# Mixture of 32 experts behind an attention layer: the widest and the narrowest expert visited last instead of second

## The chip, the cores and the metric

One core of a Trainium2 chip runs the whole layer as one program. The metric is device time in microseconds (us) of one execution; lower is better. The engines are named as in the profile: PE (TensorE matmuls), PEld (its weight loads), DVE (VectorE), ACT (ScalarE), POOL (GpSimd), SP (SyncE, which issues most DMAs).

## What is computed

A decoder layer for 1024 tokens of width 1024: an input projection, grouped attention beside a gated MLP, an output projection, then a mixture of experts. The change touches only the mixture:

```python
logits = (xt @ w_router + b_router).astype(jnp.float32)
top_val, top_idx = lax.top_k(logits, TOP_K)          # 4 of 32 experts for each token
gate = jax.nn.softmax(top_val, axis=-1)
...
def expert_block(args):
    e, tok, g = args
    xb = x_pad[tok]
    h = xb @ w_gate_up[e] + b_gate_up[e]             # 1024 -> 2048, columns interleaved
    h_glu = jnp.minimum(h[:, 0::2], SWIGLU_LIMIT)
    h_lin = jnp.clip(h[:, 1::2], -SWIGLU_LIMIT, SWIGLU_LIMIT)
    a = h_glu * jax.nn.sigmoid(SWIGLU_ALPHA * h_glu) * (h_lin + 1.0)
    return ((a @ w_down[e] + b_down[e]) * g[:, None]).astype(x.dtype)
...
y = jnp.zeros((N + 1, D), x.dtype).at[tok_buf].add(out.reshape(P, D))
```

Each token's four results are added onto its row of the output. All weights are float32 in HBM, 12 MB for each expert.

## The kernel before

**Rooms.** Experts are ranked by how many tokens chose them, on the device. The program is fixed, so the expert of rank r gets a room of `ROOM[r]` columns: 320 for rank 0, 256 for rank 1, then 240, 232, 208 and so on down to 72 for rank 30 and 64 for rank 31; 160 at rank 12, 152 at 13 and 14, 136 at 15 to 17, 120 at 19. Below, "expert 0" is the expert of rank 0. The number of the expert itself is read from a table when its weights are loaded. (A loop behind the last expert takes tokens that found no room; it makes no pass here.)

**Two streams.** `visits` (line 37) makes two lists: ranks 0 to 15 as the wide stream, ranks 31 down to 16 as the narrow one; from each it takes the element at place `FIRST = 12` (expert 12, room 160, and expert 19, room 120) and puts it first. So the wide stream is 12, 0, 1, 2, ..., 11, 13, 14, 15, and the narrow one 19, 31, 30, 29, ..., 20, 18, 17, 16. An expert is six products, four with the gate-up weights ("gu") and two with the down weights ("dn"); `pieces` (line 1925) lists them for a stream, with the next expert's first gu ahead of the present one's dn. `seq` (line 1934) takes products from the two streams by turns, the wide one three products ahead, so the last three products of the program are of the narrow stream's last expert.

**One product.** It has two halves. For each, SP loads 1 MB of weights into one of five float32 buffers (`raw`, line 1773; four of them are called xw in the trace), ACT writes the float16 high part wh (line 1780), DVE the low part wl (line 1783), into one of six buffers (`ws`). PE then does 48 matmuls for the half, four blocks of 12 (lines 1826 to 1828): wh by the two halves of x, wl by one, with as many columns as the room has. Accumulators sit in six PSUM banks. Behind a gu block DVE clamps (line 1841), ACT applies the gelu (1846), DVE multiplies (1849), ACT writes the high half of `a` (1852) and POOL the low half by a subtraction (1854); the dn products read `a`. Behind a dn block ACT adds the bias (`ott`, 1877), PE turns the result back to token rows (1894), ACT scales the rows by the gate (`orow`, 1897), and behind the second dn POOL starts an indirect DMA that adds the rows onto the output (1904). These scatters wait for one another.

**Rows in.** A room has one to three row tiles of at most 128 rows (three for room 320, two from 136 to 256, one up to 128): a one-hot matrix by DVE (1701), a pick by PE (1708), an indirect gather by POOL (`xg`, 1722), then PE transposes (1752) which ACT (1759) and DVE (1757) move out of two PSUM banks into a part of the arena `xar`. 51 row tiles in all. Arena parts are given out round robin in visiting order; a new part waits for those that it overlaps.

**Who sets the order.** Every step goes into `Plan` with a cost and a due time that follows its place in `seq`; `Plan.run` (line 198) plays the engines and writes each engine's instructions in the order in which it would start them. Each engine then runs its own list strictly in that order. So another order of experts makes another list for every engine.

Of the kernel before, what the change touches and what calls it, by code (L numbers as in the profile page):

```python
# [36 lines left out]
def visits(room):  # L37


    n = len(room)  # L40
    small, large = list(range(n - 1, n // 2 - 1, -1)), list(range(n // 2))
    return [[r.pop(FIRST)] + r for r in (large, small)]


CO = 128
FIRST = 12
# [210 lines left out]
def layer_kernel(ctx: ExitStack, tc: tile.TileContext, x, norm1_g, w_in, q_norm_g, k_norm_g, cmp_pos,  # L257
# [3 lines left out]
    nc = tc.nc  # L261
    dbg = dbg or {}
    streams = visits(room)
    order = [r for pair in zip(*streams) for r in pair]
    ctx.enter_context(tc.manual_schedule())
# [1781 lines left out]
```

## Time and profile before

| what | value |
|---|---|
| three runs | 1961.02 us median (1959.91 to 1964.04) |
| the profiled execution | 1960.88 us, its span 1959.1 us |
| PE busy | 1865.3 us, 95% of the span |
| DVE busy | 1653.5 us, 84% |
| ACT busy | 1468.2 us, 75% |
| POOL busy | 783.0 us, 40% |
| read from HBM | 450.94 MB |
| expert stage | from about 640 us to the end |

The span runs from the first to the last instruction in the trace; the time of the execution is a little longer. Busy time counts instructions, not waits; the wide view of PE's occupation says little about single waits, for which the groups of waits and the timeline are better.

### The profile page before, as it was taken

To read this page: it belongs to the slowest core of one execution; us is meant where nothing else is said; L and a number is where in the kernel's file an instruction comes from. 1 tells how busy PE (TensorE), PEld (TensorE's weight loads), DVE (VectorE), ACT (ScalarE), POOL (GpSimd) and SP (SyncE) were. 2 spreads that over 40 slices of the span, in tenths; PEclk is the share of its full clock that TensorE was granted. 3 is DMA by queue.
4 is the path that set the end of the run, shared out by engine and by line. 5 is a ranking of instruction groups with operands and counts; after the bars stand their busy time and mean duration, and the time that the engine had idled before them with its cause. 6 is when DMAs were issued, how large, how long until landed. Compare 5 with 4: busy or idle time off the path is not lost.

```text
span 1959.1 us, 60049 instructions
## 1 busy us (share of the span) xinstructions
PE 1865.3 (95%) x25170; PEld 1708.0 (87%) x25170; DVE 1653.5 (84%) x2844; ACT 1468.2 (75%) x2310; POOL 783.0 (40%) x667
## 2 busy tenths in 40 slices
PE   7999999898996999999999999999999999999996
PEld 6898777666655898899999999999999999999995
DVE  5577887778777898798998999999999999999893
ACT  6566878757554675777877888788888888888883
POOL 0111112345551454344344443353444535455432
PEclk9999999999996999999999999999999999999998
DMA  4320102221125998899999999999999999999993
GB/s 162 84 60 12 45 12 65 87 71 45 66 76 191 299 342 275 282 328 322 336 332 331 339 350 356 338 354 358 363 352 352 350 359 355 351 356 365 361 348 90
DMA packets 244775, 485.88 MB, mean 248 GB/s; under 512 B 20034, under 2 KB 29394, under 8 KB 244498
## 3 DMA queue, kind: packets, MB, share of 16 engines
q1 hardware_dynamic: 230658, 441.19, 64.2%
q0 software_dynamic: 12800, 40.79, 9.2%
q8 instruction: 199, 3.26, 0.7%
q14 instruction: 78, 0.64, 0.1%
q10 hardware_dynamic: 1040, 0.00, 0.0%
HBM read 450.94 MB, written 31.00 MB: 246 GB/s over the span
## 4 chain that ended last, share of the span: by engine, by line
PE 75%; DVE 9%; DMA 7%; ACT 5%; issue 3%; POOL 1%; SPq 0%; DVEq 0%; POOLq 0%; ACTq 0%
PE g L1826 16%; PE g L1827 16%; PE g L1828 16%; PE s L468 3%; PE s L469 3%; PE s L470 3%; DVE par L939 3%; DMA xw<-in_w_gate_up_dram 2%; PE b L1894 2%; PE b L976 2%; PE o L996 2%; DVE wl L1783 2%; DMA raw<-in_w_gate_up_dram 2%; ACT wh L1780 2%; PE b L1752 1%
## 5 line engine op out<-in xcount | busy, mean ns | idle before, releaser
L1826 PE MATMUL g<-xar,wh 128*128 128x88 f16 (+21 forms) x4096 | 770.8, 229 | 0.5 <-ACT ott L1877 0.5
L1827 PE MATMUL g<-xar,wh 128*128 128x88 f16 (+21 forms) x4096 | 771.0, 229 | 0.0
L1828 PE MATMUL g<-xar,wl 128*128 128x88 f16 (+21 forms) x4096 | 770.5, 229 | 0.1
L1783 DVE SCALAR_TENSOR_TENSOR wl<-xw,wh 128x2048 f16<-128x2048 f32 x308 | 714.4, 2326 | 40.2 <-ACT wh L1780 34.6
L1780 ACT ACTIVATE wh<-xw 128x2048 f16<-128x2048 f32 x308 | 626.4, 2036 | 157.2 <-PE g L1827 86.9
L1827 PEld LDWEIGHTS <-wh 128*128 128x128 f16 x6144 | 600.4, 98 | 15.9 <-issue 4.8
L1826 PEld LDWEIGHTS <-wh 128*128 128x128 f16 x6144 | 600.8, 98 | 10.7
L1828 PEld LDWEIGHTS <-wl 128*128 128x128 f16 x6144 | 600.3, 98 | 11.0 <-DVE wl L1783 0.3
L1854 POOL TENSOR_TENSOR aar<-t,aar 128x136 f16<-128x136 f32 (+21 forms) x256 | 360.1, 1423 | 469.1 <-ACT aar L1852 441.9
L1826 PE MATMUL g<-aar,wh 128*128 128x120 f16 (+21 forms) x2048 | 385.4, 229 | 3.8 <-DVE t L1841 3.8
L1828 PE MATMUL g<-aar,wl 128*128 128x120 f16 (+21 forms) x2048 | 385.4, 229 | 0.0
L1827 PE MATMUL g<-aar,wh 128*128 128x120 f16 (+21 forms) x2048 | 385.4, 229 | 0.0
L1841 DVE TENSOR_SCALAR t<-g,bias 128x120 f32<-128x120 f32 (+20 forms) x512 | 170.8, 364 | 32.5 <-PE g L1828 22.4
L1780 ACT ACTIVATE wh<-raw 128x2048 f16<-128x2048 f32 x76 | 154.8, 2037 | 39.6 <-PE g L1827 21.5
L1904 POOL DMA_INDIRECT out_dram<-orow,ix x51 | 124.8, 2447 | 147.7 <-ACT orow L1897 84.4
L1783 DVE SCALAR_TENSOR_TENSOR wl<-raw,wh 128x2048 f16<-128x2048 f32 x76 | 175.4, 2308 | 8.3 <-ACT wh L1780 7.7
L1722 POOL DMA_INDIRECT xg<-xn_d,ix x51 | 128.0, 2510 | 117.2 <-PE g L1828 47.2
L468 PE MATMUL s<-wh,xw 128*128 128x256 f16 (+1 forms) x576 | 158.2, 275 | 1.2 <-DVE mx L939 1.1
L469 PE MATMUL s<-wl,xw 128*128 128x256 f16 (+1 forms) x576 | 158.1, 275 | 0.0
L470 PE MATMUL s<-wh,xw 128*128 128x256 f16 (+1 forms) x576 | 158.0, 274 | 0.0
L1025 POOL TENSOR_TENSOR ob<-ob 128x512 f32<-128x512 f32 x32 | 40.7, 1270 | 191.9 <-DVE ob L1009 164.9
L1849 DVE SCALAR_TENSOR_TENSOR t<-t 128x136 f32<-128x136 f32 (+21 forms) x256 | 100.4, 402 | 18.1 <-ACT t L1846 15.1
(380 smaller groups left out, 2942.0 us busy)
## 6 DMA issues: line engine op xcount, KB each, us to landing
xw<-in_w_gate_up_dram SPq DMA_DIRECT2D x205, 1024.0 KB
xw<-in_w_down_dram SPq DMA_DIRECT2D x103, 1024.0 KB
raw<-in_w_gate_up_dram SPq DMA_DIRECT2D x51, 1024.0 KB
raw<-in_w_down_dram SPq DMA_DIRECT2D x25, 1024.0 KB
wr<-in_w_in_dram SPq DMA_DIRECT2D x16, 512.0 KB
xs<-in_x_dram SPq DMA_DIRECT2D x8, 512.0 KB
wr<-in_w_out_dram SPq DMA_DIRECT2D x8, 512.0 KB
x<-in_x_dram SPq DMA_DIRECT2D x8, 512.0 KB
```

What stands on the lines that cost most here:

```text
L468: mm(o, xa, wh, start=(k == 0), stop=False)
L469: mm(o, xa, wl, start=False, stop=False)
L470: mm(o, xb, wh, start=False, stop=(k == KD - 1))
L1722: nc.gpsimd.indirect_dma_start(out=xg.t[:w], out_offset=None, in_=xn_d, in_offset=bass.IndirectOffsetOnAxis(ap=ix.t[:w, 0:1], axis=0))
L1780: nc.scalar.activation(ws.v[0], raw_.v, AF.Copy, scale=SW)
L1783: nc.vector.scalar_tensor_tensor(ws.v[1], raw_.v, SW, ws.v[0], op0=ALU.mult, op1=ALU.subtract)
L1826: mm(o, wh, xa, start=(kh == 0 and k == 0), stop=False)
L1827: mm(o, wh, xb, start=False, stop=False)
L1828: mm(o, wl, xa, start=False, stop=(kh == 1 and k == 3))
L1841: nc.vector.tensor_scalar(t.t[:, s, :c], ps[s].t[:, :c], self.bias(2 * h + s), m, op0=ALU.add, op1=o)
L1854: plan.op("pool", 0.9 + c / 440, lambda: nc.gpsimd.tensor_tensor(out=self.a[:, h, 1], in0=t.t[:, 1, :c], in1=self.a[:, h, 0], op=ALU.subtr ...
L1904: self.plan.op("pool", 2.0, lambda: nc.gpsimd.indirect_dma_start(out=out, out_offset=bass.IndirectOffsetOnAxis(ap=ix.t[:w, 0:1], axis=0), ...
```

## The change

```diff
 def visits(room):
...
     n = len(room)
     small, large = list(range(n - 1, n // 2 - 1, -1)), list(range(n // 2))
-    return [[r.pop(FIRST)] + r for r in (large, small)]
+    return [[r.pop(FIRST)] + r[1:] + r[:1] for r in (large, small)]
```

The streams become 12, 1, 2, ..., 11, 13, 14, 15, 0 and 19, 30, 29, ..., 20, 18, 17, 16, 31. A blank line is added too, so each line of the changed kernel has a number one higher than before.

At the start of the expert stage, on ACT, the rows of the second wide expert are moved into the arena (xar) between weight conversions (wh), gelus (t) and writes of `a` (aar). Before:

```order
L1759 ACTIVATE xar<-b 128x8x112
L1852 ACTIVATE aar<-t 128x160
L1780 ACTIVATE wh<-xw 128x2048
L1759 ACTIVATE xar<-b 128x8x112
L1852 ACTIVATE aar<-t 128x160
L1780 ACTIVATE wh<-xw 128x2048
L1759 ACTIVATE xar<-b 128x8x96
```

After:

```order
L1760 ACTIVATE xar<-b 128x8x128
L1853 ACTIVATE aar<-t 128x160
L1847 ACTIVATE t<-t 128x160
L1781 ACTIVATE wh<-xw 128x2048
L1760 ACTIVATE xar<-b 128x8x128
```

Three tiles (112, 112 and 96 rows of expert 0) have become two of 128 (expert 1).

At the end, on ACT, with buffer numbers: conversions (wh), bias steps of dn results (ott), scalings of finished rows (orow), gelus (t). Before, the last conversion and what follows:

```order
L1897 ACTIVATE orow_34728<-b_34970,gtt_31880 80x512
L1897 ACTIVATE orow_34744<-b_34975,gtt_31899 56x512
L1846 ACTIVATE t_34993<-t_34993 128x136
L1780 ACTIVATE wh_35026<-xw_119 128x2048
L1846 ACTIVATE t_35009<-t_35009 128x136
L1852 ACTIVATE aar_8989<-t_34993 128x136
L1852 ACTIVATE aar_8989<-t_35009 128x136
L1846 ACTIVATE t_35125<-t_35125 128x136
```

After, the last three conversions and what stands among them:

```order
L1781 ACTIVATE wh_34906<-xw_119 128x2048
L1878 ACTIVATE ott_34864<-g_34821,bias_32128 128x320
L1781 ACTIVATE wh_34988<-xw_119 128x2048
L1898 ACTIVATE orow_34767<-b_34991,gtt_31883 112x512
L1898 ACTIVATE orow_34773<-b_34996,gtt_31890 112x512
L1847 ACTIVATE t_34973<-t_34973 128x64
L1898 ACTIVATE orow_34816<-b_35057,gtt_31949 96x512
L1847 ACTIVATE t_35054<-t_35054 128x64
L1781 ACTIVATE wh_35117<-xw_119 128x2048
L1853 ACTIVATE aar_8989<-t_34973 128x64
```

The last conversion now stands behind the three scalings of expert 0's rows and the gelus of expert 31's third product; before, both gelus of the third product of expert 16 and one of its fourth already surrounded it, with smaller tiles ahead.

At the end, on POOL: subtractions (aar) and scatters into the output (out). Before, the scatters of expert 15's two tiles and then of expert 16's:

```order
L1904 DMA out_0_dram<-orow_34728,ix_31877 1024x1024
L1854 TENSOR_TENSOR aar_8989<-t_35009,aar_8989 128x136
L1854 TENSOR_TENSOR aar_8989<-t_35125,aar_8989 128x136
L1854 TENSOR_TENSOR aar_8989<-t_35142,aar_8989 128x136
L1904 DMA out_0_dram<-orow_34744,ix_31896 1024x1024
L1904 DMA out_0_dram<-orow_35335,ix_32863 1024x1024
L1904 DMA out_0_dram<-orow_35349,ix_32884 1024x1024
```

After, those of expert 0's three tiles and of expert 31's one:

```order
L1905 DMA out_0_dram<-orow_34767,ix_31880 1024x1024
L1855 TENSOR_TENSOR aar_8989<-t_34973,aar_8989 128x64
L1855 TENSOR_TENSOR aar_8989<-t_35054,aar_8989 128x64
L1855 TENSOR_TENSOR aar_8989<-t_35160,aar_8989 128x64
L1855 TENSOR_TENSOR aar_8989<-t_35195,aar_8989 128x64
L1905 DMA out_0_dram<-orow_34773,ix_31887 1024x1024
L1905 DMA out_0_dram<-orow_34816,ix_31946 1024x1024
L1905 DMA out_0_dram<-orow_35355,ix_32898 1024x1024
```

Three scatters still stand behind the last subtraction; they are two tiles of the wide expert and one of the narrow one, where they were one and two.

## Rows read from the trace of the kernel before

**Rows 1.** The page: span, busy time (share) by engine, weight loads of line 1826

```profile
span 1959.1 us, 60049 instructions
PE 1865.3 (95%) x25170; PEld 1708.0 (87%) x25170; DVE 1653.5 (84%) x2844; ACT 1468.2 (75%) x2310; POOL 783.0 (40%) x667
...
L1826 PEld LDWEIGHTS <-wh 128*128 128x128 f16 x6144 | 600.8, 98 | 10.7
```

**Rows 2.** Stretches: length, busy (x) of PE, PEld, DVE, ACT, POOL; clock, DMA, GB/s

```profile
700.00:832.00 132.00, 130.09 (x1622) 109.05 (x1620) 110.28 (x180) 89.45 (x108) 62.37 (x29) 1.00 0.88 297
...
1200.00:1813.00 613.00, 603.79 (x9824) 601.29 (x9822) 575.89 (x687) 512.28 (x636) 294.52 (x175) 1.00 1.04 355
```

**Rows 3.** Waits of PE, 660 to 1939 us, the three largest: total, times, longest

```profile
PE b L1752 <- ACT xar L1759: 6.2, 6, 1.7
PE g L1826 <- DVE t L1841: 3.8, 3, 1.9
PE b L1752 <- DVE xar L1757: 2.6, 4, 1.5
```

**Rows 4.** The same view of 640 to 672 us, all of it

```profile
PE b L1752 <- ACT xar L1759: 2.2, 2, 1.2
PE b L1752 <- DVE xar L1757: 1.5, 1, 1.5
```

**Rows 5.** Timelines of ACT, DVE and PE near the end

```profile
1917.19 1.91 ACT L1780 ACTIVATE wh<-xw 128x2048 f16<-128x2048 f32 x1 [0.66 <-PE g L1827]
...
1923.63 2.53 DVE L1783 SCALAR_TENSOR_TENSOR wl<-xw,wh 128x2048 f16<-128x2048 f32 x1
...
1934.91 0.22 PE L1826 MATMUL g<-aar,wh 128*128 128x136 f16 x1
...
1938.62 1.37 PE L1894 MATMUL b<-ident,ott 128*80 128x128 f32 x8
```

**Rows 6.** Timeline of POOL from 1924 us, and one piece of the last chain

```profile
1924.22 3.26 POOL L1904 DMA_INDIRECT out_dram<-orow,ix  x1 [0.20 <-issue]
1926.99 1.92 POOL L1854 TENSOR_TENSOR aar<-t,aar 128x136 f16<-128x136 f32 x3
1931.44 1.45 POOL L1904 DMA_INDIRECT out_dram<-orow,ix  x1 [2.53 <-DMA out_dram<-orow,ix]
1940.55 1.43 POOL L1904 DMA_INDIRECT out_dram<-orow,ix  x1 [7.67 <-ACT orow L1897]
1946.20 1.45 POOL L1904 DMA_INDIRECT out_dram<-orow,ix  x1 [4.21 <-DMA out_dram<-orow,ix]
...
1936.49 0.87 PE b L1894 x8
```

**Rows 7.** Timeline of PE: a product of expert 31 (96 matmuls), then expert 0

```profile
729.81 0.19 PE L1826 MATMUL g<-xar,wh 128*128 128x64 f16 x1
...
732.61 0.30 PE L1826 MATMUL g<-xar,wh 128*128 128x320 f16 x1
...
732.88 0.30 PE L1828 MATMUL g<-xar,wl 128*128 128x320 f16 x1
```

**Rows 8.** Groups by form, 660 to 1960 us: busy, mean ns, idle before

```profile
L1780 ACT ACTIVATE wh<-xw 128x2048 f16<-128x2048 f32 x300 | 609.8, 2035 | 147.1 <-PE g L1827 86.9 <-DMA xw<-in_w_gate_up_dram 27.9 <-DMA xw<-in_w_down_dram 11.0
L1877 ACT ACTIVATE ott<-g,bias 128x320 f32<-128x320 f32 x8 | 4.2, 520 | 4.0 <-PE g L1828 4.0
L1897 ACT ACTIVATE orow<-b,gtt 112x512 f32<-112x512 f32 x14 | 9.4, 685 | 0.6 <-PE b L1894 0.5
L1846 ACT ACTIVATE t<-t 128x64 f32<-128x64 f32 x8 | 1.8, 253 | 0.2 <-DVE t L1841 0.2
...
L1783 DVE SCALAR_TENSOR_TENSOR wl<-xw,wh 128x2048 f16<-128x2048 f32 x301 | 698.4, 2327 | 37.3 <-ACT wh L1780 33.0 <-PE g L1827 1.8 <-issue 1.1
L1841 DVE TENSOR_SCALAR t<-g,bias 128x64 f32<-128x64 f32 x16 | 3.9, 278 | 6.9 <-PE g L1828 4.6 <-POOL aar L1854 2.2
...
L1854 POOL TENSOR_TENSOR aar<-t,aar 128x64 f16<-128x64 f32 x8 | 12.3, 1552 | 5.0 <-ACT aar L1852 5.0
```

## The prediction

> **What bounds the kernel now.** I looked first at the busy shares [rows 1], then at stretches of the expert stage (from about 640 us on) [rows 2], then at what TensorE waited for there [rows 3, 4]. What is to be seen: in both stretches shown PE is busy for over 98%, and its three largest kinds of wait between 660 and 1939 us add up to 12.6 us, 6.2 + 2.6 of them transposes that wait for ACT or DVE to empty a bank [rows 3]. So the stage is paced by TensorE's column count, and a new order of the same experts changes no column. The DMA engines are full as well in 1200 to 1813 us (355 GB/s), and are not in 700 to 832 us (297 GB/s), which is the stretch in which expert 0 (room 320) and expert 31 (room 64) run [rows 2]. That doesn't make the early stretch a reserve for the later one: the converted weights sit in a ring of six half products, so PE can never be more than six halves ahead. The last half of the program shows a usual lead: its conversion ended at 1926.16 (1923.63 + 2.53), PE began on it at 1934.91, 8.75 us later [rows 5].
>
> What lies at the ends is therefore what the move can change: how the stage fills, and how it drains. At the end PE's last expert matmul gives way to the transposes at 1938.62 [rows 5]; two scatters into the output follow, started at 1940.55 and 1946.20, the second held until the first has landed [rows 6]; the span ends at 1959.1 [rows 1], 12.9 us after the last scatter starts. The profiled execution took 1960.88 us, 1.78 us more than its span and 0.14 us under the median of the runs (1961.02), so I work on its span and add 1.78.
>
> **The change part by part.** Nothing is added or removed: 384 half products, 51 row tiles with their gathers and scatters stand in both programs. The order listings show the move really happens on every engine.
>
> *Middle.* Experts 1 to 11 and 13 to 15 with their partners keep their neighbours; each pair comes earlier by what experts 0 and 31 take on PE, six products each, 6 x (96 x 0.136 + 2.80) = 95 us by [rows 7], under the same limits. I price this at zero: the cover is the lead of 8.75 us or so per half, and if that were gone the price would be waits of the kind in [rows 3]. In the arena for the rows of x, expert 0 lands at columns 0 to 320, on the places of experts 18, 14 and 17, which are done two pairs earlier; no wait there.
>
> *Start.* The second pair is now 256 and 72 wide. Expert 0's three row tiles no longer pass through PE, ACT and DVE at 653 to 667 us, expert 1's two do. Three waits of PE there, 2.2 + 1.5 = 3.7 us, stand before transposes [rows 4]: the gain is at most 3.7 us. Against it, PE reaches the next products sooner while weights arrive no sooner. Two halves of expert 0's first product cover the supply for 2 x 48 matmuls of 0.136 us (two steps at 320 columns take 732.88 - 732.61 = 0.27) [rows 7]; at 256 columns, by the ratio of columns, a fifth less: 2.6 us less cover, all of which could turn into waiting. And the three tiles of expert 0 are now transposed late, between matmuls of 136 columns, in a stretch where PE, too, waits for ACT's evictions now and then (six times in all, the longest 1.7, [rows 3]). So this part lies between -3.7 and +2.6 + 1.7 = +4.3. I take 0, since each side has one clear row and neither reaches the other's end.
>
> *End.* This is the part with a sign. Let T be the moment when PE finishes expert 0's last product. Behind T, PE still has four products of expert 31. One of them, 96 matmuls, takes 732.61 - 729.81 = 2.80 us [rows 7], 1.40 per half; four take 11.2. Transposes behind T: three tiles of expert 0, one of 31, four matmuls each, 0.87 us for eight [rows 6], so 1.75. If PE's total is unchanged, T = 1938.62 - 12.95 = 1925.7.
>
> But a half of expert 31 needs 2.04 us on ACT and 2.33 on DVE to be converted [rows 8], against 1.40 on PE, and the ring lets the last three conversions start only at T, T + 1.4 and T + 3.7 (when PE is through with the sixth half before each: the end of expert 0, then the two halves of 31's third product, with 0.87 of transposes among them). ACT's order behind T, from the listing: conversion, one 320-wide bias step, conversion, two scalings of expert 0's rows, a gelu, the third scaling, a gelu, conversion. With 1.91 for a conversion of the down kind [rows 5], 0.52, 0.685 and 0.25 [rows 8] that is 3 x 1.91 + 0.52 + 3 x 0.685 + 2 x 0.25 = 8.8. DVE converts that half to T + 11.1 (2.33). Behind this conversion, in DVE's order, stand the last two clamps of expert 31's fourth product (0.28 each), with the two multiplications, a gelu and a copy on ACT, and POOL's subtraction. Five of these short steps follow one another, 1.3 us at 0.25 to 0.28 each [rows 8], and the subtraction at 0.64 (three in 1.92 us when DVE is quiet [rows 6]) to 1.55 (the mean at 64 columns [rows 8]). So the last subtraction ends at T + 13.1 to 14.0; I take T + 13.5. PE wants its result at 5.6 + 1.3 + 1.4 + 0.7 = T + 9.0, and waits 4.5 us.
>
> That PE wait is not the price, because POOL's queue decides the end. Its order is: scatter of expert 0's first tile, the last four subtractions, the scatters of expert 0's second and third tile and of 31. The first can go at about T + 5. The second stands behind the subtractions: T + 13.5. From scatter start to scatter start, quiet, 1946.20 - 1940.55 = 5.65 us [rows 6]: third at T + 19.2, last at T + 24.8. With the 12.9 us that follow, the span ends at T + 37.7 = 1963.4, against 1959.1: **+4.3 us**. Bounds: if the subtractions were done by PE's own pace, the chain of scatters starts at T + 5 and the last at T + 22: +1.5. If 112-row scatters step by 7.2 us (the spacing 1931.44 - 1924.22, 80 and 56 rows under load [rows 6]) and subtractions take their mean: 1.5 x 2 + 0.5, +7.9.
>
> [...] The trace spaces matmuls of 64 columns by 2.80 / 96 = 0.029 us, although each brings a weight load that is 0.098 long [rows 1, 7]. [...]
>
> Sum: 0 for the middle, 0 for the start, +4.3 for the end: a span of 1963.4, and with 1.78 outside it **1965.2 us**.
>
> **The rivals.**
> A, the forecast: 1965.2, with 1962.5 to 1969 as its own range.
> B, no wait at the end: the conversions of expert 31 slip ahead of where I put them (ACT sits idle 86.9 us in all before conversions, for PE to free the ring [rows 8], so its order has air) and POOL's subtractions end by T + 9. Only the chain of four scatters remains: +1.5, 1962.5; with part of the start's gain 1961. For it: the planner put the steps so. Against it: the ring, which no order loosens.
> C, the start starves: the pair of 320 and 64 gives the weights 384 columns to cover four halves, the new one 328, and the waits of [rows 4] show how thin the supply is just before it. If the cover of 2.6 us goes fully and the late transposes wait 1.7, the sum is 1965.2 + 4.3 = 1969.5. It decides from a lead of less than 2.6 us at the first product of the second pair.
> D, faster: the end drains with one row tile (64 rows) instead of two. If expert 0's scatters are out of the way when PE ends, a single scatter follows, which drops 5.65 us from the drain: 1955.4. In the program's order two of expert 0's scatters stand behind the last subtraction, so it needs them to start by T + 2: against the order. By weight loads as PE's pace (0.098 a matmul, 4.7 us a half, 37.6 behind T) it would be so: T + 13.5 and two steps of 5.65 end before PE does. The spacing of 0.029 speaks against it. A milder form of D: the start's 3.7 us and the 1.9 us that PE waited once for a gate's DVE step [rows 3] are gained in full, with the end at its lower bound: 1961.0 - 5.6 + 1.5 = 1956.9.
> That the change does not do what it says is out: the listings show it.
>
> **How the numbers follow.** A 0.48, B 0.23, C 0.15, D 0.14 (0.02 of it for weight loads as the pace). A difference of about 0.2%, 3.9 us, is what a measurement of this kernel can tell from none; the edges are 1957.1 and 1964.9. A's centre is almost on the upper edge: 0.27 of it above, 0.21 within. Slower: 0.27 + 0.15 = 0.42, and a little of B with late transposes, 0.03: 0.45. Same: 0.21 + 0.20 = 0.41. Faster: 0.14. The range leaves out the full D and the far side of C: 1957.0 (mild D) to 1971.0 (C and a slower chain of scatters).
>
> **What would show each step right or wrong.** In the changed profile PE's last product of 320 columns should end near 1925.7; a PE wait of 3 to 5 us for POOL or the gate should follow some 9 us later, in front of down matmuls of 64 columns; three scatters should stand back to back at 5.6 to 7 us, the last starting 24 to 26 us behind the end of expert 0. If the 320-wide product ends later than 1928, the start or the middle lost time (C); if before 1923, they gained (D). If the scatters step by much more than 7 us, or PE waits over 1 us in several middle pairs where it didn't before, my pricing of the middle at zero is wrong, since then DMA, not PE, sets the pace there.

## The result, and the profile after

The changed kernel takes 1975.54 us (median of 7 runs, 1971.37 to 1979.61), the kernel before 1965.99 beside it (7 runs, 1959.91 to 1968.25): a ratio of 1.0053, with a 95% interval of 1.0036 to 1.0071. A second set gave 1.0067 (1.0042 to 1.0091). It is slower, as the likeliest sign had it, but by some 10 to 13 us, not 4, and the time lies outside the range. The profiled execution took 1976.08 us.

The part ahead of the experts, which the change doesn't touch, ends at another time in every trace: the fourth half product starts at 642.61 us in the first trace of before and at 646.01 in that of after (643 to 650 in the others). From there to the end it is 1316.5 and 1315.2 us in two traces of before, 1328.2 and 1328.7 in two of after: 12.6 us more. The rows below are read from that start on.

Page of the changed kernel: span and busy times, then the chain that ended last, by engine; the second fence has that line of the kernel before.

```profile
span 1974.2 us, 60042 instructions
PE 1873.9 (95%) x25170; PEld 1715.6 (87%) x25170; DVE 1648.7 (84%) x2844; ACT 1468.7 (74%) x2310; POOL 781.3 (40%) x667
...
PE 70%; DVE 10%; DMA 9%; ACT 6%; issue 3%; POOL 1%; DVEq 0%; SPq 0%; POOLq 0%; ACTq 0%
```

```profile
PE 75%; DVE 9%; DMA 7%; ACT 5%; issue 3%; POOL 1%; SPq 0%; DVEq 0%; POOLq 0%; ACTq 0%
```

Against [rows 1], the instructions and the shares are the same; in the chain 5% of the span have moved from PE to DMA, ACT and DVE. That share is a loose measure (PE has 74% in the second trace of before and 63% in that of after). Where the time went is told by the gaps on PE. I took the start of each PE instruction from the trace, subtracted the usual step of its shape (56 ns at 128 columns, 136 at 320), and added up what is over 0.12 us, by stages, in us. The first column ends with the last product of the second wide expert (0 before, 1 after); the four rows with light loads belong to the experiments:

| trace | start, first two pairs | experts 2 to 11 | 13, 14 | 15 to 17 | 0 and 31 at the end | all |
|---|---|---|---|---|---|---|
| before | 6.6 | 8.6 | 2.7 | 0.9 | - | 18.8 |
| before, second trace | 5.1 | 8.2 | 3.3 | 0.6 | - | 17.2 |
| after | 6.6 | 7.1 | 4.7 | 6.1 | 2.8 | 27.3 |
| after, second trace | 6.6 | 8.8 | 4.4 | 5.7 | 2.5 | 28.0 |
| before, light loads | 4.4 | 0.2 | 0.0 | 0.9 | - | 5.5 |
| after, light loads | 4.6 | 0.0 | 0.2 | 1.0 | 3.1 | 8.9 |
| after, light late (first) | 6.3 | 5.9 | 2.7 | 1.0 | 3.1 | 19.0 |
| after, light late (second) | 6.5 | 9.2 | 1.9 | 1.0 | 2.9 | 21.5 |

On average of two traces the start lost 0.8, experts 2 to 11 lost nothing (8.4 before, 8.0 after), 13 and 14 lost 1.5, which is no more than one stage differs between two traces of the same kernel, and the largest item, 5.2, is the stage of experts 15 to 17, whose order against each other nobody changed.

In the start two things cancel. PE's waits ahead of the second wide expert's row tiles fell from over 4 us to 2.0. But 1.9 to 2.6 us of others stand later in the second pair in each of the eleven traces with expert 1 second, where of the six with expert 0 one has 2.1 us and the rest 0.6 at most. In after, from 770 to 781 us:

```profile
PE g L1827 <- DVE t L1842: 1.8, 2, 1.4
```

By the timeline these clamps stand on DVE behind some 60 short steps on the table of tokens that found no room, 766.4 to 773.5 us, and one conversion; no run moved these steps.

PE's waits in the stage of 15 to 17, in after (1691 to 1806 us), then in before (1789.5 to 1939, its end); columns are total, times, longest:

```profile
PE b L1753 <- ACT xar L1760: 2.1, 2, 1.3
PE g L1827 <- DVE t L1842: 1.0, 1, 1.0
PE g L1827 <- ACT ott L1878: 0.5, 1, 0.5
PE b L1753 <- DVE xar L1758: 0.3, 1, 0.3
PE b L1895 <- DVE xar L1758: 0.2, 1, 0.2
```

```profile
PE b L1752 <- DVE xar L1757: 0.3, 1, 0.3
PE b L1894 <- DVE xar L1757: 0.2, 1, 0.2
```

The view blames ACT and DVE. ACT's own timeline in that stage of after shows what they were waiting for:

```profile
1775.12 2.06 ACT L1781 ACTIVATE wh<-xw 128x2048 f16<-128x2048 f32 x1 [2.61 <-DMA xw<-in_w_gate_up_dram]
...
1780.51 1.91 ACT L1781 ACTIVATE wh<-raw 128x2048 f16<-128x2048 f32 x1 [0.35 <-DMA raw<-in_w_down_dram]
1782.33 0.30 ACT L1853 ACTIVATE aar<-t 128x136 f16<-128x136 f32 x1
1782.54 0.30 ACT L1847 ACTIVATE t<-t 128x136 f32<-128x136 f32 x1
1783.56 1.91 ACT L1781 ACTIVATE wh<-xw 128x2048 f16<-128x2048 f32 x1 [0.73 <-DMA xw<-in_w_down_dram]
...
1788.03 2.10 ACT L1781 ACTIVATE wh<-xw 128x2048 f16<-128x2048 f32 x1 [1.93 <-DMA xw<-in_w_gate_up_dram]
...
1791.47 2.08 ACT L1781 ACTIVATE wh<-xw 128x2048 f16<-128x2048 f32 x1
1793.43 0.93 ACT L1760 ACTIVATE xar<-b 128x896 f16<-128x896 f16 x1
```

Conversions (wh) stand in ACT's fixed order, and the first four shown wait for a weight load, 5.6 us in all within 13 us. What stands behind them comes late: the first of expert 0's three row tiles (xar) leaves its bank at 1793.43 only, and PE, which needs the bank for the second tile, waits 1.3 us. In this stage the conversions waited for loads as follows, first in after (1691 to 1806 us), then in before (1789.5 to 1892):

```profile
ACT wh L1781 <- DMA xw<-in_w_gate_up_dram: 8.5, 6, 2.6
ACT wh L1781 <- DMA xw<-in_w_down_dram: 3.9, 4, 1.5
```

```profile
ACT wh L1780 <- DMA xw<-in_w_gate_up_dram: 2.3, 3, 1.1
ACT wh L1780 <- DMA xw<-in_w_down_dram: 0.2, 1, 0.2
```

The same two rows sum to 7.1 us in the second trace of after and to 3.6 in that of before. Over all of the time from 660 us, ACT's conversions in after:

```profile
L1781 ACT ACTIVATE wh<-xw 128x2048 f16<-128x2048 f32 x300 | 609.7, 2035 | 163.6 <-PE g L1828 88.2 <-DMA xw<-in_w_gate_up_dram 30.7 <-DMA xw<-in_w_down_dram 20.5
```

The same group waited 27.9 + 11.0 us for loads in [rows 8] and 30.7 + 20.5 here. But the second traces have 49.2 in before and 49.7 in after, so this total doesn't tell the two kernels apart; the single stage does.

Stretches of both kernels (columns as in [rows 2]; the last two are the DMA engines' share and GB/s): first after, the stage of 15 to 17 and the last pair; then before, the two halves of its last stage.

```profile
1691.00:1806.00 115.00, 110.67 (x1826) 108.94 (x1824) 105.72 (x133) 93.86 (x120) 52.22 (x34) 1.00 1.03 349
1863.00:1935.00 72.00, 72.00 (x797) 57.47 (x795) 46.29 (x43) 46.73 (x57) 16.53 (x12) 1.00 0.70 231
```

```profile
1789.00:1866.00 77.00, 76.47 (x1265) 75.89 (x1263) 70.41 (x83) 65.39 (x82) 36.67 (x22) 1.00 1.05 363
1866.00:1938.00 72.00, 72.00 (x1187) 71.91 (x1185) 56.76 (x61) 55.50 (x79) 27.40 (x20) 1.00 0.81 264
```

Two half products of 136 columns take PE 2 x 48 x 0.059 = 5.7 us and eat 2.1 MB of weights: 370 GB/s, before any row is gathered. With all DMA engines busy (1.03 to 1.05) the chip moved 349 to 363, less than such a pair needs. So pairs this narrow run at the speed of their loads. A last pair is let off: no successor has its rows gathered (1.6 MB for experts 0 and 31) and moved by ACT and DVE, and its own loads end early (in before the last weight packet ends at 1919.2, 19 us before PE is through with its last product). Before, the narrowest pair had this place, and moved 264 GB/s in its last 72 us with PE never waiting. Now the widest pair has it, which needs 48 x (0.136 + 0.029) = 7.9 us for the same 2.1 MB, and in its stretch above (1863 to 1935 us) PE waits for nothing and ACT for no load.

### The profile page after: what moved, and what is told of

The parts are those of the page before. It is cut to its first block, busy times and chain, and to the rows that moved or that the text cites. A ratio compares the mean times of both kernels' runs of the same rounds, so it can differ in the third digit from the quotient of the medians.

```text
span 1974.2 us, 60042 instructions
## 1 busy us (share of the span) xinstructions
PE 1873.9 (95%) x25170; PEld 1715.6 (87%) x25170; DVE 1648.7 (84%) x2844; ACT 1468.7 (74%) x2310; POOL 781.3 (40%) x667
## 4 chain that ended last, share of the span: by engine, by line
PE 70%; DVE 10%; DMA 9%; ACT 6%; issue 3%; POOL 1%; DVEq 0%; SPq 0%; POOLq 0%; ACTq 0%
PE g L1827 15%; PE g L1828 15%; PE g L1829 15%; DMA xw<-in_w_gate_up_dram 5%; PE s L469 3%; PE s L470 3%; PE s L471 3%; DVE wl L1784 3%; DVE par L940 3%; ACT wh L1781 2%; PE b L977 2%; PE o L997 2%; PE b L1895 2%; DMA raw<-in_w_gate_up_dram 2%; PE s L1338 1%
## 5 line engine op out<-in xcount | busy, mean ns | idle before, releaser
L1855 POOL TENSOR_TENSOR aar<-t,aar 128x120 f16<-128x120 f32 (+21 forms) x256 | 363.3, 1437 | 501.5 <-ACT aar L1853 480.3
L1905 POOL DMA_INDIRECT out_dram<-orow,ix x51 | 117.5, 2304 | 142.4 <-ACT orow L1898 84.2
L1723 POOL DMA_INDIRECT xg<-xn_d,ix x51 | 132.2, 2593 | 103.6 <-DVE ix L1715 36.1
L985 DVE SCALAR_TENSOR_TENSOR pl<-b,ph 128x512 f16<-128x512 f32 (+1 forms) x148 | 98.3, 685 | 20.2 <-ACT ph L981 19.0
```

What stands on the lines that cost most here:

```text
L1723: nc.gpsimd.indirect_dma_start(out=xg.t[:w], out_offset=None, in_=xn_d, in_offset=bass.IndirectOffsetOnAxis(ap=ix.t[:w, 0:1], axis=0))
L1855: plan.op("pool", 0.9 + c / 440, lambda: nc.gpsimd.tensor_tensor(out=self.a[:, h, 1], in0=t.t[:, 1, :c], in1=self.a[:, h, 0], op=ALU.subtr ...
L1905: self.plan.op("pool", 2.0, lambda: nc.gpsimd.indirect_dma_start(out=out, out_offset=bass.IndirectOffsetOnAxis(ap=ix.t[:w, 0:1], axis=0), ...
```

## Experiments

All kernels are compared with runs of the kernel before on the same chip.

### The same pair at other places

Third from last (e1) and eighth (e2), against the changed kernel:

```diff
-    return [[r.pop(FIRST)] + r[1:] + r[:1] for r in (large, small)]
+    return [[r.pop(FIRST)] + r[1:13] + r[:1] + r[13:] for r in (large, small)]   # e1
+    return [[r.pop(FIRST)] + r[1:7] + r[:1] + r[7:] for r in (large, small)]     # e2
```

> Experts 0 and 31 are visited third from last (12, 1, ..., 11, 13, 0, 14, 15), so the program ends with the same two pairs as before. The changed kernel lost about 10 us: about 5 behind expert 0's last product, as worked out, and 6.6 us ahead of it. Theory L (late place): the 6.6 us come from three row tiles of expert 0 being transposed late, among the narrow products of the last stages. Here the end is as before (0), the late tiles stand among 152 columns: +3 to +6, ratio 1.0015 to 1.003. Theory S (lost second place): what is lost is expert 0 as cover of the start, 6 us wherever it goes: ratio 1.003. Theory E (all of it is the very end, the 6.6 us included, since PE's last products starve there): ratio 1.000.

> Experts 0 and 31 are visited eighth (12, 1, ..., 6, 0, 7, ...). L: the place is neither early nor late, products around it are 184 columns wide, so nothing is lost: ratio 1.000 (within 0.001). S: 6 us are lost since the second place is given up: ratio 1.003. E: ratio 1.000. A ratio under 0.999 would say that the second place itself was bad, by the waits of 3.7 us ahead of expert 0's transposes.

Measured: e1 1973.25 us, ratio 1.0046 (1.0031 to 1.0062); e2 1974.77, 1.0048 (1.0029 to 1.0067). Theories L and E fall as I had them: with the end as before, and even in the middle, the move costs what it costs at the end. Theory S came nearer in size, but not in place: the start of both loses hardly more than before (6.0 to 7.0 us of gaps in the first two pairs, against 5.1 to 6.6). The waits lie beside the moved pair. In e2 from 1144 to 1489 us:

```profile
PE g L1827 <- ACT ott L1878: 3.5, 2, 1.9
PE b L1753 <- ACT xar L1760: 3.2, 2, 2.6
PE g L1827 <- DVE t L1842: 3.0, 3, 1.5
```

The wide stream is three products ahead, so expert 31's last three (64 columns) run beside the next wide expert: 184 columns in e2, 5.2 us for two halves (403 GB/s), 152 in e1, 4.6 us (460 GB/s). In the kernel before it was expert 1 with 256: 6.6 us, 316 GB/s, and there is no wait in that pair. (These are estimates from the steps in the trace of before: 0.029 us at 64 columns, 0.066 at 152, 0.079 at 184, 0.109 at 256; a half is 48 of them.)

### One half of the pair alone

Against the kernel before:

```diff
+    return [[large.pop(FIRST)] + large, [small.pop(FIRST)] + small[1:] + small[:1]]   # e3, 31 last
+    return [[large.pop(FIRST)] + large[1:] + large[:1], [small.pop(FIRST)] + small]   # e4, 0 last
```

> Only expert 31 is visited last in the narrow stream; expert 0 stays second. The end has two tiles of expert 15 and one of 31 to scatter, where it had two and two before. L and E: conversions of 31's halves (2.0 on ACT, 2.3 on DVE against 1.4 on PE) hold the last product up by 2 to 4 us, one scatter less gives back 5.7: ratio 0.998 to 1.000. S: the second pair is 320 and 72 columns, more cover than before: the same 0.998 to 1.000. If what costs at the end is expert 31's narrow halves, 1.002 or more.

> Only expert 0 is visited last in the wide stream; expert 31 stays second, beside expert 1. The narrow stream ends with expert 16, whose halves (3.1 us on PE) are longer than their conversions, so PE should not wait at the end; five scatters (three of expert 0, two of 16) end the program where the changed kernel had four. L: late transposes +6, end +5 to +8: ratio 1.0055 to 1.007. S: +6 for the start and the same end: 1.0055 to 1.007. If expert 31's narrow halves are what costs: under 1.003.

Measured: e3 1967.20, ratio 1.0009 (0.9995 to 1.0024), between what the theories gave; e4 1987.79, 1.0114 (1.0092 to 1.0136), 22 us, more than any theory gave. Moving one list shifts all partners: in e3 every wide expert runs beside one that is a rank wider, in e4 a rank narrower (often 8 columns). PE's gaps from expert 2 to the last product of 11 fall from 8.5 to 5.2 us in e3 and rise to 17.4 in e4, which has 15.3 more behind. Eight columns of 280 are 3% of PE's time for a pair of halves: by these two runs enough to go from fed to starved. In e4 the granted clock also fell to 0.50 four times, for 3.4 us each, at PE waits of 1.9 to 3.4 us; 13.4 busy us at that clock cost some 6 us more, an estimate from the steps of 64 columns in the changed kernel (0.053 us at a clock of 0.51, 0.029 at 1.00). E3 pays at its end for expert 31 behind expert 15 (waits from 1890 us on, in an execution of 1977.13 us, 9.9 above the median):

```profile
PE g L1828 <- POOL aar L1855: 8.6, 2, 5.5
PE g L1827 <- ACT ott L1878: 2.6, 1, 2.6
PE g L1829 <- DVE wl L1784: 2.3, 1, 2.3
```

### Lighter weight loads everywhere

Everything stays in its order, and each load fetches three of its four blocks of rows from the second pair on:

```diff
-                nc.sync.dma_start(t, w[...][:, 512 * kh:512 * kh + 512, ...]
+                seen.append(h)
+                m = 4 if len(seen) <= 24 else 3
+                nc.sync.dma_start(t[:, :m], w[...][:, 512 * kh:512 * kh + 128 * m, ...]
```

> The kernel before, but from the second pair on every weight load fetches only three of its four blocks of 128 rows; conversions, products and their order are as they were, the fourth block holds old data, so the output is not the reference's. It asks what the speed of the weight loads costs. Theory D (from about 1250 us on weights arrive only just as fast as PE eats them, and what looks like waits for ACT and DVE are conversions that waited for a load): nearly all of the 12.6 us of PE waits behind 660 us go, and the kernel is 6 to 12 us faster than before, ratio 0.994 to 0.997. Theory O (the waits are in the planner's order of ACT and DVE, loads have nothing to do with them): ratio 0.999 to 1.001.

> The changed kernel with the same lighter loads (three of four blocks from the second pair on; output not the reference's). D: the 6.6 us lost ahead of expert 0's last product go, only the end's 5 us stay: 4 to 6 us above the kernel before with light loads. O or a loss by late transposes: 9 to 12 us above it, as with full loads.

> The kernel before once more, for a second trace of it beside the others on this chip: ratio 1.000, and waits of PE behind the start of the expert stage within 3 us of the first trace if such waits belong to the order of the program; further off if they are chance.

> The changed kernel once more: ratio 1.004 to 1.007, the PE waits in its last pairs (1.4 us more in the pairs of 160 and 152 columns than the same pairs had before) there again within 1 us each, if they belong to the program; spread elsewhere if they are chance.

Measured: before with light loads 1952.06 (ratio 0.9946, 0.9925 to 0.9967), after with light loads 1955.94 (0.9959, 0.994 to 0.9978); before again 1965.17 (1.0011, 0.9997 to 1.0025), after again 1977.41 (1.0067). With full loads the two kernels of this set are 12.2 us apart, with light ones 3.9, the size of the end. The gaps of experts 2 to 11 go from 8.6 to 0.2 and from 7.1 to 0.0 (table); those of the second pair stay (2.1 us), so they aren't waits for loads. ACT's conversions of after, light:

```profile
L1783 ACT ACTIVATE wh<-xw 128x2048 f16<-128x2048 f32 x300 | 609.5, 2035 | 144.7 <-PE g L1830 108.2 <-issue 10.3 <-ACT wh L1783 6.9
```

No wait for a load is left among its largest; ACT waits for PE instead, as the prediction thought it did everywhere. Theory D holds; that lighter weight loads also leave more room to the row gathers isn't told apart. The repeats put bounds on chance: the sum of gaps comes again within 1.6 us and single stages within 1.7 (2.5 and 3.3 for the two light late traces, which are of one kernel), though which product waits in the middle differs from trace to trace.

### Lighter loads at one place only

The changed kernel with light loads only for half products 318 to 372 (twice), then e2's and e1's order with light loads around the moved pair:

```diff
+                m = 3 if 318 <= len(seen) <= 372 else 4    # e9, e15 (order: changed kernel)
+                m = 3 if 136 <= len(seen) <= 246 else 4    # e13 (order: e2)
+                m = 3 if 318 <= len(seen) <= 366 else 4    # e14 (order: e1)
```

> The changed kernel with lighter weight loads (three of four blocks of 128 rows; output not the reference's) only for the half products 318 to 372 of 384, that is from late in the pair of expert 14 to the first products of experts 0 and 31. Two traces of the changed kernel have PE waits of 5.7 and 6.1 us in the stage of experts 15 and 16, where the kernel before, which has no pair behind that stage, has 0.6 to 0.9. Theory D (a pair in the middle waits for loads, the last pair doesn't): these waits fall under 1.5 us and the whole is 4 to 6 us faster than the changed kernel: ratio to before 1.002 to 1.0035. If late transposes of expert 0's three tiles are the cause by themselves: the waits stay, ratio 1.005 to 1.007.

> The changed kernel with lighter loads for half products 318 to 372 once more. D: PE waits in the stage of experts 15 and 16 of about 1 us again (5.7 to 6.1 with full loads); the whole 4 to 6 us faster than the changed kernel's 1975 to 1977, ratio to before 1.0025 to 1.004. Otherwise 1.005 to 1.0065.

> The kernel with experts 0 and 31 eighth (ratio 1.0048), with lighter weight loads (three of four blocks of 128 rows; output not the reference's) for the half products 136 to 246 alone, from the pair ahead of 0 and 31 to two pairs behind. In its trace PE waits 11.4 us from product half 144 to 240, against 3 to 4 us for the same experts in the kernel before. Theory D: behind the wide pair expert 31's last three products (64 columns) run beside expert 7's (184), 248 columns for two halves, and PE outruns the loads; with lighter loads these waits go under 2 us and the ratio falls to 0.9985 to 1.001. If the pair's place costs by something else (late transposes, banks, order): waits stay, 1.004 to 1.005.

> The kernel with experts 0 and 31 third from last (ratio 1.0046), with lighter loads for the half products 318 to 366 alone, around expert 31's last three products beside expert 14 (64 and 152 columns). Its trace has PE waits of 6.6 us there, one of 5.1 in front of a product that waited for a bias step of ACT. Theory D: these go under 1 us, ratio 1.0005 to 1.002. Otherwise 1.004 to 1.005.

Measured: e9 1973.93 (1.0043, 1.0025 to 1.006), e15 1971.92 (1.0034, 1.0019 to 1.0048), e13 1961.92 (0.9982, 0.997 to 0.9994), e14 1968.11 (1.0012, 0.9999 to 1.0024). In the stage of 15 to 17 the waits of e15 (1690 to 1800 us) are two short ones, and those for ACT are gone although expert 0's tiles are transposed at the same place:

```profile
PE b L1753 <- DVE xar L1758: 0.3, 1, 0.3
PE b L1897 <- DVE xar L1758: 0.2, 1, 0.2
```

Late transposes by themselves are thus not the cause. The whole came back by some 2 to 6 us, e9 short of what I expected, e15 within it; the intervals overlap with the changed kernel's, so it is the gaps of that stage (1.0 in both traces, against 6.1 and 5.7) that carry this. In e13 PE waits for nothing between 1144 and 1489 us, and the ratio falls from 1.0048 to 0.9982, just under the range expected. In e14 the largest wait in the pair behind expert 0 goes from 4.9 to 2.4 us, less than expected; the ratio falls as expected. The trace of e14, its slowest execution, doesn't show the gain: gaps of 26.2 us in all against 25.8 in e1, with more of them in other pairs. First e1, then e14:

```profile
PE g L1827 <- ACT ott L1878: 4.9, 1, 4.9
```

```profile
PE g L1829 <- ACT ott L1880: 2.4, 1, 2.4
```

### Another pair last, and the end by itself

The first two against the kernel before, the third against the changed one:

```diff
+    return [[r.pop(FIRST)] + r[:7] + r[8:] + r[7:8] for r in (large, small)]                              # e11
+    return [[large.pop(FIRST)] + large, [small.pop(FIRST)] + small[:12] + small[13:] + small[12:13]]      # e10
+            plan.op("dve" if c == 64 else "pool", ..., (nc.vector if c == 64 else nc.gpsimd).tensor_tensor(   # e12
```

> Experts 0 and 31 stay second; experts 7 and 24 (184 and 104 columns) are visited last. Theory D: the stage of experts 15 and 16 pays 4 to 5 us, since now a pair stands behind it, and the early part gives back up to 1 (those two no longer stand in the middle); the end has one row tile of the narrow expert instead of two, one scatter step of 5.65 us less: 0 to -3 in all, ratio 0.998 to 1.000. If what the changed kernel lost belongs to experts 0 and 31 alone: no loss at 15 and 16, ratio 0.996 to 0.9975.

> The kernel before, with expert 18 (128 rows, one row tile) as the last of the narrow stream instead of expert 16 (136, two tiles): ..., 20, 17, 16, 18. Everything else as before. If each scatter that stands behind the last product costs its step of 5.65 us, the end is one step shorter: 1958 to 1960 where before has 1964, ratio 0.997 to 0.998. If something else sets the end (the first scatter's own landing, the work of PE): 0.9995 to 1.001. Halves of 128 columns take PE 2.7 us, more than their conversion, so no PE wait is expected of them.

> The changed kernel, but expert 31's low halves of a are written by DVE instead of POOL, so that POOL's queue holds only scatters behind expert 0's last subtraction; nothing else is moved. If POOL's queue sets the end, as predicted (second scatter held behind the last subtraction until T + 13.5), the second scatter starts one step of 5.65 to 6 us behind the first, at T + 11, and the end comes 2 to 3 us sooner: ratio to before 1.004 to 1.005 where the changed kernel has 1.0053 to 1.0067; the PE wait of 2.5 us ahead of expert 31's down product shrinks under 1.5. If the end is set by PE's last product: no change, 1.0055 to 1.0065.

Measured: e11 1967.75 (1.0005, 0.9992 to 1.0018). Both pairs tried behind 15 and 16 make them wait: the stage of 15 to 17 has 4.9 us of gaps in this trace, where before has 0.9 and 0.6, and no gain is left of the shorter end.

E10 is faster than both kernels: **1959.22 us, ratio 0.9973 (0.9961 to 0.9984)**. Its end on POOL:

```profile
1930.59 1.43 POOL L1904 DMA_INDIRECT out_dram<-orow,ix  x1 [0.16 <-issue]
...
1936.23 1.46 POOL L1904 DMA_INDIRECT out_dram<-orow,ix  x1 [3.37 <-DMA out_dram<-orow,ix]
1943.16 1.57 POOL L1904 DMA_INDIRECT out_dram<-orow,ix  x1 [5.48 <-ACTq L1995]
```

One scatter follows PE's last product (about 1941), where two did in [rows 6]: one step, 5.65 us, for a measured 5.3.

E12 refutes a step of mine: 1981.29 (1.0086, 1.0061 to 1.0111), not faster. First the end of the changed kernel on POOL, then that of e12:

```profile
1940.67 3.61 POOL L1905 DMA_INDIRECT out_dram<-orow,ix  x1 [9.73 <-ACT orow L1898]
...
1947.64 0.30 POOL L1855 TENSOR_TENSOR aar<-t,aar 128x64 f16<-128x64 f32 x1 [0.26 <-POOL aar L1855]
1949.13 1.47 POOL L1905 DMA_INDIRECT out_dram<-orow,ix  x1 [1.19 <-DMA out_dram<-orow,ix]
1955.24 1.43 POOL L1905 DMA_INDIRECT out_dram<-orow,ix  x1 [4.64 <-DMA out_dram<-orow,ix]
1961.24 1.43 POOL L1905 DMA_INDIRECT out_dram<-orow,ix  x1 [4.57 <-DMA out_dram<-orow,ix]
```

```profile
1942.91 3.60 POOL L1905 DMA_INDIRECT out_dram<-orow,ix  x1 [15.82 <-ACT orow L1898]
1951.65 1.46 POOL L1905 DMA_INDIRECT out_dram<-orow,ix  x1 [5.14 <-ACT ott L1878]
1958.30 1.42 POOL L1905 DMA_INDIRECT out_dram<-orow,ix  x1 [5.19 <-DMA out_dram<-orow,ix]
```

With nothing of expert 31 left in POOL's queue the second scatter still starts 8.74 us behind the first (8.46 in the changed kernel). In both, POOL is through with its work before: the first scatter is itself slow. Its last packet ends at 1948.54 in the changed kernel and at 1950.56 in e12, 7.9 and 7.7 us behind its start. The view of e12 names a bias step of ACT, which ended 0.8 us after that packet, so at most this much is not the first scatter's. PE's wait ahead of the down product stays too (2.4 us; 2.3 in the changed kernel), so it isn't POOL's either. E12 is slower still than the changed kernel (the intervals overlap), but its trace loses that ahead of the end: from the fourth half product to expert 0's last it takes 5.2 us longer. Some 2 of these are gaps, and some 3, estimated as for e4, a fall of TensorE's clock to 0.50 at a PE wait of 2.6 us, in columns as above:

```profile
1668.80:1675.60 6.80, 6.44 (x59) 6.41 (x59) 5.84 (x12) 4.51 (x8) 2.90 (x2) 0.50 1.05 384
```

The granted clock of the changed kernel is 1.00 there. Why e12 had that wait isn't shown.

## Why the prediction was wrong, point by point

**What bounds the kernel: half right.** That the stage is paced by PE's columns holds as long as two halves side by side have many columns: in the first trace of before the waits of the middle begin with 192 and 96 at 1257 us. From there on the loads hold PE up now and then: with lighter ones 8.4 us of its gaps go. The prediction saw full DMA engines in 1200 to 1813 us [rows 2] and took the lead of 8.75 us [rows 5] as proof that PE is fed. The lead was there throughout (9 to 12 us on average of 24 halves in both kernels behind the second pair, more beside expert 0, and 8.4 or more in the stage of 15 to 17); the waits don't come from missing weights for PE but from ACT's and DVE's fixed orders, in which a conversion that waits for its load holds back the small steps behind it. The waits [rows 3] named ACT's evictions; behind these stood, in [rows 8], 38.9 us in which ACT's conversions waited for loads, and these I read as harmless.

**Middle, priced at zero: the step that failed.** For experts 2 to 11 zero was right (8.4 us of gaps before, 8.0 after, averages of two traces). But the sentence went on to experts "13 to 15 with their partners keep their neighbours", and the last pair did not: it had no successor, and got one. That costs 5.2 us at 15 to 17; 1.5 more at 13 and 14 may be chance. The condition I had written down, that waits grow where DMA sets the pace, came true there, and the mark for it as well: expert 0's last product ended at 1935.62, 3.4 of it from the part ahead of the experts, so 1932.2 against 1925.7 and the limit of 1928.

**Start, -3.7 to +4.3, taken as 0: right within its bounds.** The gaps of the first two pairs went from 6.6 and 5.1 to 6.6 in both traces: 0.8 lost, not for the reasons given but by the waits for DVE in the second pair. Rival C, which gave 1969.5, had the nearer total by the wrong place: the start didn't starve for loads, since light ones left these waits as they were.

**End, +4.3: right in size, wrong in a reason.** From T to the end of the span it is 38.6 us, predicted 37.7. Scatters at T + 5.1, 13.5, 19.6 and 25.6 were predicted at 5, 13.5, 19.2 and 24.8. But the second was to be held by the last subtraction, which ended at T + 12.3; it was held by the first scatter's landing, and e12 shows that POOL's queue made no difference. PE waited 2.3 us, not 4.5, for a clamp behind the last conversion. With 0.9 for the longer end and 6.5 for the later T the sum is 4.3 + 0.9 + 6.5 = 11.7 us, the difference of the first two traces from the fourth half product on; the table explains 5.7 of the 6.5 (24.5 us of gaps ahead of the end, against 18.8).

**Rival B and D** needed the scatters out of the way earlier, and fell with the first one's 8.5 us. Weight loads as PE's pace fell too: PE's halves of expert 31 step by 0.029 us at the end as well, and by 0.053 only where the clock fell.

## What to carry to other kernels

When the trace names a fast engine as the releaser, look one step further back in that engine's own order: if something ahead of the named step waits for a load, the load may be the cause, however long the mean lead is, and a run with lighter loads tells. The last place in a pipeline is free of prefetch for a successor (before moved 264 GB/s there, and PE never waited), so it should go to the stage that is shortest of bandwidth, not to the largest; and where two streams run side by side with an offset, judge every place by the two that really overlap. At the very end count the dependent scatters behind the last product: one row tile less was worth 5.3 us in e10.

## What was not expected of the hardware

A scatter of 112 rows that POOL starts beside DVE's conversions (from 1940.62 to 1946.08 in the changed kernel) kept POOL for 3.60 to 3.88 us in the six traces of this order, against 1.42 to 1.48 when DVE was quiet, and the next could start only 8.1 to 9.8 us after it, against 5.9 to 7.8 for the later steps of these traces. Of the 51 scatters in the changed kernel's trace, 6 have no conversion of DVE beside their first 1.4 us and kept POOL for 1.43 to 1.47 us; 40 have over 0.5 us of one beside them and kept it for 1.44 to 4.02, half of them for 2.80 or more. No run here took DVE's work away at that place, so the reason stays open.

TensorE's clock fell after PE's single wait of 2.3 us at the end: the granted clock is 0.51 from 1947.5 to 1951, just behind a stretch in which PE was busy for 1.17 of 3.5 us. Matmuls of 64 columns start 0.053 us apart there instead of 0.029 at 1.00, which makes some 1.4 us in all; the kernel doesn't pay it, since the last scatter waits for the one before. The price is paid where PE sets the pace, as in e12 and e4. Falls of 3.4 or 6.8 us stand at waits in the traces of e1, e2, e3, e14 and e15 too, and none in the middle of the expert stage in the two traces of before and the two of after (1.00 from 645 to 1940 us in the first of before, and to 1945 in that of after). The rows give length, busy time of PE, PEld, DVE, ACT and POOL, clock, DMA share and GB/s:

```profile
1944.00:1947.50 3.50, 1.17 (x41) 1.08 (x38) 2.92 (x5) 0.84 (x5) 2.81 (x4) 1.00 0.82 118
1947.50:1951.00 3.50, 3.35 (x68) 3.24 (x64) 0.00 (x0) 1.26 (x5) 1.78 (x2) 0.51 0.10 20
```

No stretch of 70 us or more shown here moved more than 363 GB/s, and the largest of the 40 slices of 49 us on the changed kernel's page is 375.
